# Two products of the 256-token matmuls in one instruction of 512 moving columns

## The chip, the cores and the metric

The kernel runs on one core of a Trainium2 chip. The metric is the device time of one execution in microseconds (us). Before the change the median of three timed executions is 2486.03 us (2485.91 to 2488.45). Differences within 0.2% (about 5 us) are taken as no change.

## The reference

A model of two blocks on 256 tokens, all in float32. The first block (`first_block`) is attention over 8 heads beside a pooled branch, an output projection, and a feed-forward part with a causal convolution of width 3. The second block puts 16 meta tokens ahead of the 256 (272 in all) for an "even" layer (a state-space branch and a convolution branch), and has an "odd" layer of neighbourhood attention.

```
h = rms_norm(x, attn_norm_g)                      # 256 tokens, width 2048
proj = h @ w_in                                   # q, k, v and p
a = moba_attention(q, k, v, rel_bias)
m = multiscale_pool(p, pool_w, pool_scale)
x = x + concatenate([a, m]) @ w_out

u = rms_norm(x, ffn_norm_g) @ w_up                # 2048 -> 2 * 5632
y = conv_b + sum(conv_w[i] * shifted(u, i))       # three taps
gate, val = split(y)
x = x + (silu(gate) * val) @ w_down               # 5632 -> 2048
...
x = even layer on 272 tokens; x = odd layer: queries and gates of 256 tokens, keys and values of 272
```

## The kernel before

Activations are kept transposed: features on the 128 partitions, tokens along the free axis. So a projection to 128 output features is a sum over feature tiles k (16 for a width of 2048, 11 for a quarter of the feed-forward width) of W_k^T x_k, where the 128x128 weight tile stands in TensorE and the tokens (256 or 272 columns) move through it.

Float32 precision is kept with two parts: each factor is a sum of a high and a low part of type f32r. `split_act` makes the parts of an activation, `xh` (ScalarE copy) and `xl` (VectorE subtraction), in two tiles from a pool of 79 slots (`slot`). `split_next` makes the parts of the weights, `wH` (ScalarE, L184) and `wL` (L185, on GpSimd for the first half of most chunks, else on VectorE). `products` then issues three matmuls for each k into one accumulator: wH with xh (L225), wH with xl (L226), wL with xh (L227). The fourth product, of both low parts, is left out.

The weights stream in a fixed order (`plan`), one chunk for each 128 outputs. Three chunks are in flight in SBUF and four half chunks of parts exist, so the split of the half chunk that comes three ahead waits until TensorE is through with one. Accumulators (`acc`) rotate through three PSUM banks. What follows a chunk reads its accumulator on VectorE: in the feed-forward part `u = acc * r` (L589), then ScalarE makes `y` (L591) and VectorE adds two taps (L592, L594); for the `val` half the product with the gate (L603) and the split for the next projection (L263, L264). The down and output projections add the accumulator to the residual (L571, L621, L1104).

Chunks with 256 moving columns are: p (8 chunks), the pooled products `mix` (16 k in all), w_out (16), gate and val (88), down (64 of 11 k each), oq, oz and o_out (16 each). The q, k and v chunks of the attention have the tokens as weights (`rows`), and the whole even layer and ok, ov of the odd layer move 272 columns. A scheduling layer puts each engine's instructions in order ahead of time, engine by engine, with the code's order as priority and a model of its own for what is ready; each engine runs its list strictly in that order. In the even layer much work runs "in the background" between the chunks.

Of the kernel before, what the change touches and what calls it, by code (L numbers as in the profile page):

```python
# [10 lines left out]
F32 = mybir.dt.float32  # L11
# [23 lines left out]
# columns of the per-feature parameters  # L35
# [10 lines left out]
# columns of the phases' constants  # L46
# [11 lines left out]
class Kernel:  # L58
    def __init__(self, ctx, tc, A, out):
        self.ctx, self.tc, self.nc, self.A, self.out = ctx, tc, tc.nc, A, out  # L60
        self.bg = deque()
        self.live = []
# [8 lines left out]
    # ---------------------------------------------------------------- tiles  # L71
    NSLOT = 79
    WIDE = 5

    def slot(self, dt=F32, name="slot"):
        return self.ap_.tile([P, S2], dt, name=name, tag="slot", bufs=self.NSLOT)

# [11 lines left out]

    def gp(self):  # L90
        return self.pp.tile([P, 512], F32, name="gp", tag="gp", bufs=3)
# [10 lines left out]
    # ------------------------------------------------------- weight streaming  # L102
# [55 lines left out]
    def load_next(self, parts=1):  # L158
        """the next chunk; yields before each of its parts."""
# [10 lines left out]
    def split_next(self):  # L170
        """the next piece of the weights as two f32r parts whose sum is exact."""
# [26 lines left out]
    def chunk(self, key, ahead=1):  # L198
# [6 lines left out]
        while self.n_split < min(i + 1 + ahead, n):  # L205
            # ahead of the work in the background, where there is much of it
# [1036 lines left out]
```

## Time and profile before

| | |
|---|---|
| median of three timed executions | 2486.03 us (2485.91 to 2488.45) |
| span of the profiled execution, first to last instruction | 2484.6 us |
| TensorE matmul (PE) busy | 2422.9 us (98%) |
| VectorE (DVE) busy | 1681.3 us (68%) |
| ScalarE (ACT) busy | 1254.7 us (50%) |
| GpSimd (POOL) busy | 1092.7 us (44%) |
| mean granted TensorE clock | 0.988 |

The page does not time what lies around the span; the median of the timed executions is 1.4 us above the span. Busy time of PE counts any stretch in which a matmul is in the array; matmuls overlap in it, so a busy PE can still be made faster by fewer or denser matmuls.

### The profile page before, as it was taken

How to read it: one execution, taken by the hardware profiler on the slowest of the kernel's cores; microseconds unless marked ns; L12 is line 12 of the kernel's file. 1: busy time of each engine (PE TensorE's matmuls, PEld its weight loads, DVE VectorE, ACT ScalarE, POOL GpSimd, SP SyncE). 2: the span in 40 equal slices, each digit the busy share in tenths (PEclk: the TensorE clock that was granted, in tenths of full speed). 3: DMA queues.
4: the chain of work that ended last, by engine and by line, in shares of the span. 5: the costliest groups of instructions: out<-in, count | busy, mean ns of one | idle time of the engine just before them, and what ended most of it. 6: DMA issues, size and time to landing. Idle time of an engine off the chain costs nothing. (4 is left out here: it accounts for less than half of the span.)

```text
span 2484.6 us, 48431 instructions
## 1 busy us (share of the span) xinstructions
PE 2422.9 (98%) x19742; PEld 2379.5 (96%) x19742; DVE 1681.3 (68%) x2917; ACT 1254.7 (50%) x1914; POOL 1092.7 (44%) x505
## 2 busy tenths in 40 slices
PE   8999999999999999999989998988999999999998
PEld 8998999999999999999989997878999999999998
DVE  6566466667666667889999988888767644443443
ACT  6564455554554554554445564744544444444553
POOL 1133444445445445644458765444334333333443
PEclk9999999999999999999999998999999999999999
DMA  8545655557657656865545464554666544444553
GB/s 284 185 140 195 231 192 184 182 176 231 219 175 228 224 177 223 256 206 176 171 146 194 168 205 146 183 165 151 214 231 211 187 157 169 171 167 170 197 187 119
DMA packets 116415, 471.62 MB, mean 190 GB/s; under 512 B 17376, under 2 KB 54496, under 8 KB 72416
## 3 DMA queue, kind: packets, MB, share of 16 engines
q1 hardware_dynamic: 94880, 443.87, 53.4%
q10 hardware_dynamic: 21312, 24.67, 2.8%
q8 instruction: 154, 2.52, 0.4%
q14 instruction: 69, 0.57, 0.1%
HBM read 448.94 MB, written 19.54 MB: 189 GB/s over the span
## 5 line engine op out<-in xcount | busy, mean ns | idle before, releaser
L225 PE MATMUL acc<-xh,wH 128*128 128x256 f32 (+1 forms) x5856 | 1678.1, 287 | 17.8 <-DVE c L755 8.9
L227 PE MATMUL acc<-xh,wL 128*128 128x256 f32 (+1 forms) x5856 | 1669.1, 285 | 2.7 <-POOL wL L185 2.4
L226 PE MATMUL acc<-xl,wH 128*128 128x256 f32 (+1 forms) x5856 | 1671.6, 285 | 0.2 <-DVE xl L267 0.2
L185 POOL TENSOR_TENSOR wL<-raw,wH 128x1024 fp32r<-128x1024 f32 (+1 forms) x435 | 1041.2, 2396 | 1316.0 <-ACT wH L184 1212.2
L184 ACT ACTIVATE wH<-raw 128x1024 fp32r<-128x1024 f32 (+1 forms) x838 | 832.7, 998 | 854.3 <-PE acc L226 641.8
L225 PEld LDWEIGHTS acc<-xh,wH 128*128 128x128 f32 x5856 | 1110.0, 190 | 27.2 <-ACT dt L739 9.1
L227 PEld LDWEIGHTS acc<-xh,wL 128*128 128x128 f32 x5856 | 1109.0, 189 | 4.8 <-POOL wL L185 4.0
L226 PEld LDWEIGHTS acc<-xl,wH 128*128 128x128 f32 x5856 | 1109.2, 189 | 1.2 <-DVE xl L267 0.3
L185 DVE TENSOR_TENSOR wL<-raw,wH 128x1024 fp32r<-128x1024 f32 (+2 forms) x403 | 579.6, 1440 | 142.1 <-ACT wH L184 137.1
L665 DVE SCALAR_TENSOR_TENSOR cvp<-u,prm,cvp 128x264 f32<-128x264 f32 (+14 forms) x480 | 210.0, 488 | 0.3
L264 DVE TENSOR_TENSOR xl<-y,xh 128x256 fp32r<-128x256 f32 x44 | 98.7, 2243 | 25.0 <-ACT xh L263 25.0
L238 PE MATMUL acc<-wH,xh 128*128 128x256 f32 x384 | 108.6, 285 | 5.8 <-ACT xh L266 5.8
L589 DVE TENSOR_TENSOR u<-acc,r 128x256 f32<-128x256 f32 x88 | 36.7, 418 | 111.2 <-PE acc L227 109.1
L240 PE MATMUL acc<-wH,xl 128*128 128x256 f32 x384 | 108.9, 285 | 0.9 <-DVE xl L267 0.9
L239 PE MATMUL acc<-wL,xh 128*128 128x256 f32 x384 | 107.5, 282 | 0.0
L238 PEld LDWEIGHTS acc<-wH,xh 128*128 128x128 f32 x384 | 72.8, 190 | 5.8 <-ACT xh L266 5.8
L290 DVE TENSOR_TENSOR nacc<-nacc,sq 128x272 f32<-128x272 f32 (+1 forms) x103 | 70.9, 688 | 9.8 <-ACT sq L279 8.6
L240 PEld LDWEIGHTS acc<-wH,xl 128*128 128x128 f32 x384 | 72.8, 190 | 2.3 <-DVE xl L267 1.9
L849 POOL TENSOR_TENSOR e<-e 128x128 f32<-128x128 f32 x64 | 47.8, 769 | 57.3 <-DVE e L847 55.4
L239 PEld LDWEIGHTS acc<-wL,xh 128*128 128x128 f32 x384 | 72.6, 190 | 0.1
L761 DVE SCALAR_TENSOR_TENSOR gp<-c,prm,gp 128x270 f32<-128x270 f32 (+1 forms) x128 | 62.9, 496 | 3.3 <-ACT gp L757 3.1
L621 DVE TENSOR_TENSOR xw<-acc,xw 128x256 f32<-128x256 f32 x64 | 27.2, 424 | 51.3 <-PE acc L227 48.6
(231 smaller groups left out, 1456.7 us busy)
## 6 DMA issues: line engine op xcount, KB each, us to landing
raw<-in_e_w_in_dram SPq DMA_DIRECT2D x97, 1024.0 KB
raw<-in_w_up_dram SPq DMA_DIRECT2D x88, 1024.0 KB
raw<-in_o_w_in_dram SPq DMA_DIRECT2D x64, 1024.0 KB
raw<-in_w_down_dram SPq DMA_DIRECT2D x64, 704.0 KB
raw<-in_e_w_out_dram SPq DMA_DIRECT2D x32, 1024.0 KB
raw<-in_w_qkv_dram SPq DMA_DIRECT2D x21, 1024.0 KB
raw<-in_w_out_dram SPq DMA_DIRECT2D x16, 1024.0 KB
raw<-in_o_w_out_dram SPq DMA_DIRECT2D x16, 1024.0 KB
```

What stands on the lines that cost most here:

```text
L184: nc.scalar.activation(H[:, c], w[:, c], AF.Copy)
L185: eng.tensor_tensor(L[:, c], w[:, c], H[:, c].bitcast(F32), op=OP.subtract)
L225: nc.tensor.matmul(ps, wh, xh, start=k == 0, stop=False)
L226: nc.tensor.matmul(ps, wh, xl, start=False, stop=False)
L227: nc.tensor.matmul(ps, wl, xh, start=False, stop=k == n - 1)
L238: nc.tensor.matmul(ps[b], xh, H[:, o:o + 256], start=k == 0, stop=False)
L239: nc.tensor.matmul(ps[b], xh, L[:, o:o + 256], start=False, stop=False)
L240: nc.tensor.matmul(ps[b], xl, H[:, o:o + 256], start=False, stop=k == 15)
L264: nc.vector.tensor_tensor(l, x, h.bitcast(F32), op=OP.subtract)
L290: nc.vector.tensor_tensor(st["acc"], st["acc"], sq, op=OP.add)
L665: nc.vector.scalar_tensor_tensor(cps[i][:, a:b], u[i][:, a + s:b + s], self.prm_("dww", k * 16 + i), cps[i][:, a:b], op0=OP.mult, op1=OP.add)
L761: nc.vector.scalar_tensor_tensor(y[:, a:b], t[:, a + d:b + d], self.prm_("ecw", k * 32 + c), y[:, a:b], op0=OP.mult, op1=OP.add)
```

## The change

The two parts of an activation now lie in one tile of two halves (`twin`, [128, 2, 272]). With 256 tokens the matmul of wH takes both halves as its moving operand, 512 columns, and writes the two halves of a PSUM bank (`acc2`); the matmul of wL with the high part adds 256 columns to the first half. The halves are added when the result is read (`add2`): a ScalarE copy of the second half and a VectorE addition of the first, or, where a residual is added anyway, two VectorE additions. The form with 272 tokens stays at three matmuls, since 544 columns don't fit a bank. Tiles of one part share a twin by twos (`slot`), and the pool has 39 twins (78 halves) in place of 79 slots.

```diff
-    NSLOT = 79
+    NSLOT = 39
-    def slot(self, dt=F32, name="slot"):
-        return self.ap_.tile([P, S2], dt, name=name, tag="slot", bufs=self.NSLOT)
+    def twin(self, dt=F32, name="twin"):
+        return self.ap_.tile([P, 2, S2], dt, name=name, tag="slot", bufs=self.NSLOT)
+    def slot(self, name="slot"):
+        if self.half is None:
+            t = self.twin(name=name)
+            self.half = t[:, 1]
+            return t[:, 0]
+        t, self.half = self.half, None
+        return t
+    def acc2(self):
+        return self.pp.tile([P, 2, S1], F32, name="acc", tag="acc", bufs=3)
...
-            xh, xl = pairs[k]
+            x = pairs[k]
             wh, wl = self.weights(W, k if at is None else at[k])
-            nc.tensor.matmul(ps, wh, xh, start=k == 0, stop=False)
-            nc.tensor.matmul(ps, wh, xl, start=False, stop=False)
-            nc.tensor.matmul(ps, wl, xh, start=False, stop=k == n - 1)
+            if len(ps.shape) == 3:
+                nc.tensor.matmul(ps, wh, x, start=k == 0, stop=False, skip_group_check=True)
+                nc.tensor.matmul(ps[:, 0], wl, x[:, 0], start=False, stop=k == n - 1, skip_group_check=True)
+            else:
+                nc.tensor.matmul(ps, wh, x[:, 0], start=k == 0, stop=False)
+                nc.tensor.matmul(ps, wh, x[:, 1], start=False, stop=False)
+                nc.tensor.matmul(ps, wl, x[:, 0], start=False, stop=k == n - 1)
+    def add2(self, out, ps, x=None):
+        nc = self.nc
+        if x is None:
+            nc.scalar.copy(out, ps[:, 1])
+        else:
+            nc.vector.tensor_tensor(out, ps[:, 1], x, op=OP.add)
+        nc.vector.tensor_tensor(out, ps[:, 0], out, op=OP.add)
...
-        h = self.slot(F32R, "xh")[:, :n]
-        l = self.slot(F32R, "xl")[:, :n]
+        t = self.twin(F32R, "xhl")[:, :, :n]
+        h, l = t[:, 0], t[:, 1]
...
-                ps = self.acc()[:, :S1]
+                ps = self.acc2()
                 self.products(ps, W, [mixed[2 * g], mixed[2 * g + 1]], [4 * (g % 2) + j, 4 * (g % 2) + 2 + j])
-                mX[2 * g + j] = self.split_act(ps, S1, self.prm_("pscale", 2 * g + j))
+                t = self.work("mx")[:, :S1]
+                self.add2(t, ps)
+                mX[2 * g + j] = self.split_act(t, S1, self.prm_("pscale", 2 * g + j))
...
-            ps = self.acc()[:, :S1]
+            ps = self.acc2()
             self.products(ps, W, X)
             u = self.work("u")[:, :S1]
-            nc.vector.tensor_tensor(u, ps, r(), op=OP.mult)
+            self.add2(u, ps)
+            nc.vector.tensor_tensor(u, u, r(), op=OP.mult)
...
-                ps = self.acc()[:, :S1]
+                ps = self.acc2()
                 self.products(ps, W, K)
                 x = t[:, NM:]
-                nc.vector.tensor_tensor(x, ps, x, op=OP.add)
+                self.add2(x, ps, x)
```

p, oq and oz change as the feed-forward `u` does, w_out and o_out as the down projection.

TensorE's list, in a chunk of the feed-forward part, two of its 16 k before the change (names are out<-in with buffer numbers):

```order
L225 MATMUL acc_5859<-xh_2948,wH_5785 128x256
L226 MATMUL acc_5859<-xl_2949,wH_5785 128x256
L227 MATMUL acc_5859<-xh_2948,wL_5786 128x256
L225 MATMUL acc_5859<-xh_3027,wH_5785 128x256
L226 MATMUL acc_5859<-xl_3028,wH_5785 128x256
L227 MATMUL acc_5859<-xh_3027,wL_5786 128x256
```

The same place after it, three k (line numbers are those of the changed kernel: L242 and L243 stand in `products`):

```order
L242 MATMUL acc_4889<-xhl_2769,wH_4826 128x512
L243 MATMUL acc_4889<-xhl_2769,wL_4827 128x256
L242 MATMUL acc_4889<-xhl_2832,wH_4826 128x512
L243 MATMUL acc_4889<-xhl_2832,wL_4827 128x256
L242 MATMUL acc_4889<-xhl_2886,wH_4826 128x512
L243 MATMUL acc_4889<-xhl_2886,wL_4827 128x256
```

Each k has two matmuls in place of three, with as many columns in all.

VectorE's list in the feed-forward part, from the read of one val accumulator to the next gate's, before:

```order
L589 TENSOR_TENSOR u_5908<-acc_5859,r_4071 128x256
L185 TENSOR_TENSOR wL_5926<-raw_5849,wH_5925 128x1024
L592 SCALAR_TENSOR_TENSOR y_5910<-u_5908,prm_72,y_5910 128x255
L594 SCALAR_TENSOR_TENSOR y_5910<-u_5908,prm_72,y_5910 128x254
L603 TENSOR_TENSOR y_5910<-y_5844,y_5910 128x256
L264 TENSOR_TENSOR xl_5916<-y_5910,xh_5915 128x256
L589 TENSOR_TENSOR u_5978<-acc_5929,r_4071 128x256
```

And after the change, for a val chunk as well (L256 adds in `add2`, L622 is the product with r, L199 the weights' low part, L625 and L627 the taps, L636 the product with the gate, L293 the split):

```order
L256 TENSOR_TENSOR u_4974<-acc_4941,u_4974 128x256
L622 TENSOR_TENSOR u_4974<-u_4974,r_3637 128x256
L625 SCALAR_TENSOR_TENSOR y_4978<-u_4974,prm_72,y_4978 128x255
L627 SCALAR_TENSOR_TENSOR y_4978<-u_4974,prm_72,y_4978 128x254
L636 TENSOR_TENSOR y_4978<-y_4926,y_4978 128x256
L199 TENSOR_TENSOR wL_5045<-raw_4986,wH_5044 128x1024
L293 TENSOR_TENSOR xhl_4983<-y_4978,xhl_4983 128x256
L256 TENSOR_TENSOR u_5029<-acc_4996,u_5029 128x256
```

There is one more addition a chunk, the product with r now has both inputs in SBUF, and the weights' low part has moved from ahead of the taps to behind the product with the gate.

ScalarE's list in the even layer where the background of the state-space branch starts, before (c5 are results of the convolutions of width 5, here the last of x; cb, x0 and xt belong to the first group):

```order
L930 DMA z_a3_18377<-z_a_18375 128x272
L831 COPY cb_18398<-gp_18399 128x16
L952 ACTIVATE xw_21264<-xw_21264 128x272
L817 ACTIVATE x0_18394<-x0_18392 128x128
L764 ACTIVATE c5_18048<-gp_18042 128x272
L859 COPY xt_18411<-gp_18408 128x256
L184 ACTIVATE wH_18553<-raw_18436 128x1024
```

And after the change:

```order
L864 COPY cb_16018<-gp_16019 128x16
L892 COPY xt_16031<-gp_16028 128x256
L198 ACTIVATE wH_16176<-raw_16056 128x1024
L797 ACTIVATE c5_15594<-gp_15588 128x272
L797 ACTIVATE c5_15594<-gp_15663 128x272
L892 COPY xt_16145<-gp_16142 128x256
```

Both of the last two c5 tiles, which share a twin, are now written behind the first group; before, one was.

## Rows read from the trace of the kernel before

**Rows 1.** The page: busy time, and TensorE's granted clock in 40 slices.

```profile
span 2484.6 us, 48431 instructions
...
PE 2422.9 (98%) x19742; PEld 2379.5 (96%) x19742; DVE 1681.3 (68%) x2917; ACT 1254.7 (50%) x1914; POOL 1092.7 (44%) x505
...
PEclk9999999999999999999999998999999999999999
```

**Rows 2.** Groups of matmuls by line and shape: count, busy us, mean ns, idle before.

```profile
L226 PE MATMUL acc<-xl,wH 128*128 128x256 f32 x3280 | 925.2, 282 | 0.2 <-DVE xl L267 0.2
L225 PE MATMUL acc<-xh,wH 128*128 128x256 f32 x3280 | 924.3, 282 | 8.8 <-ACT xh L266 6.3 <-DVE xl L267 1.9 <-DVE p L538 0.5
L227 PE MATMUL acc<-xh,wL 128*128 128x256 f32 x3280 | 923.1, 281 | 0.1
```

**Rows 3.** Windows, PE alone: us, busy, matmuls, granted clock, DMA share.

```profile
400.00:980.00 580.00, 580.00 (x4900) 1.00 0.60 201
1120.00:1240.00 120.00, 120.00 (x962) 1.00 0.50 170
```

**Rows 4.** Timeline of PE in the feed-forward part: start, us.

```profile
600.10 0.28 PE L227 MATMUL acc<-xh,wL 128*128 128x256 f32 x1
600.22 0.29 PE L225 MATMUL acc<-xh,wH 128*128 128x256 f32 x1
600.34 0.28 PE L226 MATMUL acc<-xl,wH 128*128 128x256 f32 x1
600.46 0.27 PE L227 MATMUL acc<-xh,wL 128*128 128x256 f32 x1
```

**Rows 5.** PE's own waits, the longest: us in total, times, longest.

```profile
PE gp L857 <- DVE c L878: 11.6, 2, 6.5
PE acc L225 <- DVE c L755: 8.9, 1, 8.9
PE acc L225 <- ACT xh L266: 6.3, 2, 3.4
PE gp L813 <- DVE dupx L811: 5.4, 1, 5.4
PE acc L225 <- DVE xl L267: 1.9, 2, 1.4
```

**Rows 6.** Windows, all engines: PE, PEld, DVE, ACT, POOL busy; gate and val, then down.

```profile
434.80:496.90 62.10, 62.10 (x526) 62.10 (x525) 42.19 (x55) 32.77 (x44) 25.92 (x12) 1.00 0.53 182
559.00:618.00 59.00, 59.00 (x502) 59.00 (x501) 41.53 (x37) 24.44 (x33) 34.42 (x15) 1.00 0.70 224
```

**Rows 7.** Groups of VectorE by line and shape, whole span.

```profile
L589 DVE TENSOR_TENSOR u<-acc,r 128x256 f32<-128x256 f32 x88 | 36.7, 418 | 111.2 <-PE acc L227 109.1 <-ACT r L308 2.1
L264 DVE TENSOR_TENSOR xl<-y,xh 128x256 fp32r<-128x256 f32 x44 | 98.7, 2243 | 25.0 <-ACT xh L263 25.0
L603 DVE TENSOR_TENSOR y<-y 128x256 f32<-128x256 f32 x44 | 19.3, 439 | 3.3 <-ACT y L601 1.8
L185 DVE TENSOR_TENSOR wL<-raw,wH 128x384 fp32r<-128x384 f32 x64 | 139.4, 2178 | 6.0 <-ACT wH L184 2.0
L185 DVE TENSOR_TENSOR wL<-raw,wH 128x256 fp32r<-128x256 f32 x16 | 6.2, 416 | 5.0 <-ACT wH L184 5.0
```

**Rows 8.** Timelines of DVE and of POOL in the gate and val chunks.

```profile
479.15 2.42 DVE L264 TENSOR_TENSOR xl<-y,xh 128x256 fp32r<-128x256 f32 x1 [0.59 <-ACT xh L263]
481.50 0.41 DVE L589 TENSOR_TENSOR u<-acc,r 128x256 f32<-128x256 f32 x1
...
486.37 0.42 DVE L589 TENSOR_TENSOR u<-acc,r 128x256 f32<-128x256 f32 x1 [2.42 <-PE acc L227]
...
478.89 2.40 POOL L185 TENSOR_TENSOR wL<-raw,wH 128x1024 fp32r<-128x1024 f32 x1 [3.29 <-ACT wH L184]
484.58 2.41 POOL L185 TENSOR_TENSOR wL<-raw,wH 128x1024 fp32r<-128x1024 f32 x1 [3.29 <-ACT wH L184]
```

**Rows 9.** Groups of ScalarE by line and shape: a copy out of PSUM, the weights' split.

```profile
L422 ACT COPY q<-acc 128x256 f32<-128x256 f32 x8 | 3.0, 372 | 8.4 <-PE acc L240 8.4
L184 ACT ACTIVATE wH<-raw 128x1024 fp32r<-128x1024 f32 x750 | 790.5, 1057 | 842.7 <-PE acc L226 633.8 <-issue 151.9 <-PE acc L240 22.6
```

**Rows 10.** Timeline at the end: the last accumulator's addition on DVE.

```profile
2472.76 0.42 DVE L1104 TENSOR_TENSOR x<-acc,x 128x256 f32<-128x256 f32 x1 [5.27 <-PE acc L227]
2474.10 0.38 DVE L328 TENSOR_SCALAR ms<-gp 128x1 f32<-128x1 f32 x2 [0.92 <-PE gp L325]
```

**Rows 11.** Windows in the even layer, all engines as in Rows 6.

```profile
1242.30:1304.40 62.10, 53.19 (x421) 53.00 (x421) 60.99 (x108) 26.22 (x33) 32.18 (x13) 0.96 0.42 146
1490.80:1552.90 62.10, 53.53 (x361) 47.78 (x361) 52.52 (x97) 27.07 (x46) 33.32 (x23) 0.89 0.43 146
```

More of the change, by code (lines that the diff above doesn't have):

```diff
@@ L61, in __init__ @@
         self.bg = deque()
+        self.half = None
         self.live = []
@@ L236, in rows @@
             for b in blocks:
-                xh, xl = (t[:, b * P:(b + 1) * P] for t in X[k])
+                xh, xl = (X[k][:, i, b * P:(b + 1) * P] for i in range(2))
                 nc.tensor.matmul(ps[b], xh, H[:, o:o + 256], start=k == 0, stop=False)
@@ L267, in split_act @@
             nc.vector.scalar_tensor_tensor(l, x, scale, h.bitcast(F32), op0=OP.mult, op1=OP.subtract)
-        return h, l
+        return t
     def norm_begin(self, n, tail=0):
@@ L537, in attention @@
             p = self.work("p")[:, :S1]
-            nc.vector.tensor_tensor(p, ps, rf, op=OP.mult)
+            self.add2(p, ps)
+            nc.vector.tensor_tensor(p, p, rf, op=OP.mult)
             self.advance()
@@ L552, in attention @@
         K = [aX[h] for h in range(HEADS)] + [mX.get(k - 8) for k in at[8:]]
-        first = self.acc()[:, :S1]
+        first = self.acc2()
         self.products(first, W, K, at, range(10))
@@ L585, in conv @@
             W = self.chunk((kind, i))
-            ps = self.acc()[:, :S1]
+            ps = self.acc2()
             self.products(ps, W, X)
             u = self.work("u")[:, :S1]
-            nc.vector.tensor_tensor(u, ps, r(), op=OP.mult)
+            self.add2(u, ps)
+            nc.vector.tensor_tensor(u, u, r(), op=OP.mult)
             y = self.work("y")[:, :S1]
@@ L617, in down @@
                 W = self.chunk(("down", s, j))
-                ps = self.acc()[:, :S1]
+                ps = self.acc2()
                 self.products(ps, W, K)
                 x = t[:, NM:]
-                nc.vector.tensor_tensor(x, ps, x, op=OP.add)
+                self.add2(x, ps, x)
                 if last:
@@ L873, in pair @@
             m = slice(32 * i, 32 * i + 32)
-            (xh, xl), (wh, wl) = X0[t], W0[t]
+            (xh, xl), (wh, wl) = X0[t], (W0[t][:, j] for j in range(2))
             for n, (a, b) in enumerate(((xh, wh), (xh, wl), (xl, wh))):
@@ L995, in odd @@
         negm = cols(cd, CD, "neg").rearrange("p (b k) -> p b k", b=2)
-        XG = [(h[:, NM:], l[:, NM:]) for h, l in X]
+        XG = [t[:, :, NM:] for t in X]
         rg = lambda: r()[:, NM:]
@@ L1059, in odd @@
             W = self.chunk(("oq", hp))
-            ps = self.acc()[:, :S1]
+            ps = self.acc2()
             self.products(ps, W, XG)
@@ L1063, in odd @@
             q = self.work("oq")[:, :S1]
-            nc.vector.scalar_tensor_tensor(q, ps, 0.125, rg(), op0=OP.mult, op1=OP.mult)
+            self.add2(q, ps)
+            nc.vector.scalar_tensor_tensor(q, q, 0.125, rg(), op0=OP.mult, op1=OP.mult)
             kv = []
@@ L1079, in odd @@
             W = self.chunk(("oz", i))
-            ps = self.acc()[:, :S1]
+            ps = self.acc2()
             self.products(ps, W, XG)
@@ L1083, in odd @@
             t = self.work("oz")[:, :S1]
-            nc.vector.tensor_tensor(t, ps, rg(), op=OP.mult)
+            self.add2(t, ps)
+            nc.vector.tensor_tensor(t, t, rg(), op=OP.mult)
             nc.scalar.activation(t, t, AF.Silu)
@@ L1100, in odd @@
             W = self.chunk(("o_out", j))
-            ps = self.acc()[:, :S1]
+            ps = self.acc2()
             self.products(ps, W, K)
             nc.sync.dma_start(x[j], self.x[j][:, NM:])
-            nc.vector.tensor_tensor(x[j], ps, x[j], op=OP.add)
+            self.add2(x[j], ps, x[j])
             self.norm_add(st, x[j])
```

## The prediction

> **What bounds the kernel now.** I read the page first, then TensorE's groups, its windows, its waits, and last the engines beside it. The page shows TensorE's matmuls in progress during 98% of the span, at a granted clock of full level (the upper one of 1.2 and 2.4 GHz) in nearly every slice, while VectorE has 32% of the span free, ScalarE 50% and GpSimd 56% [rows 1]. That PE is busy says little, since matmuls overlap; the two views that count are PE's waits and its step. The waits come to few microseconds: the five longest are 34 us in all, and most of these stand in the even layer [rows 5], which the change leaves at three matmuls. So in the stages with 256 columns TensorE issues one matmul after another without a stop, and the time of such a stage is the number of matmuls by the step between their starts.
>
> The step can be read from windows without waits. In the feed-forward part 4900 matmuls of 256 columns fill 580 us: 118.37 ns each. In the even layer's first part 962 of 272 columns fill 120 us: 124.74 ns [rows 3]. The two differ by 6.37 ns for 16 columns, so 0.398 ns a column, and a part is left that doesn't depend on the columns: 118.37 - 256 x 0.398 = 16.5 ns. The shorter window is uncertain by one matmul, 0.13 ns, which moves the slope by 0.008. If the slope is one cycle of the 2.4 GHz level, 0.417 ns, the fixed part is 118.37 - 106.7 = 11.7 ns by the first window and 124.74 - 113.3 = 11.4 ns by the second. I take 11.6, nearest to both windows at the granted clock, and keep 16.5 as the upper bound. The duration of a row (282 ns, [rows 2]) is the way of one matmul through the array and no step.
>
> The fixed part doesn't come from the change of weights: L225 and L226 use the same wH tile one after the other, L227 another, and each step in the timeline is 0.12 us [rows 4].
>
> **What the change removes.** Each of the 3280 k of the 256-token products [rows 2] has three matmuls of 256 columns, 3 x 118.4 = 355.1 ns, and will have one of 512 and one of 256. The columns stay; one fixed part of three goes. A 512-column matmul has no row. Between the bounds: nothing saved (236.7 ns, two steps of 256) and 16.5 ns saved. By the fixed part of 11.6 it steps 213.3 + 11.6 = 224.9 ns, a k takes 343.3 ns, and the sum is 3280 x 11.6 = **38.0 us** (0 to 54 us). It lies on the path that sets the end, since these stages have hardly a wait. A chunk of 16 k goes from 5.68 to 5.49 us, one of 11 from 3.91 to 3.78.
>
> The Trainium skill bears on this (TensorE: Matmul & The Clock Gate, Back-to-back issue gap): it gives a back-to-back gap of columns by cycle plus about 2.5 ns. The rows show 11.4 to 16.5 instead, in a stream where each matmul has its own weight load; by the page's 2.5 ns the saving would be 3280 x 2.5 = 8.2 us.
>
> **What it adds.** ScalarE gets 136 copies out of PSUM (8 p, 8 mix, 88 gate and val, 16 oq, 16 oz) at 0.37 us [rows 9], 50 us. VectorE gets an addition for each of these and for the 96 residual chunks (16 + 64 + 16): 232 by 0.42 us, the price of L589, which also reads PSUM [rows 7], 97 us. ScalarE would stand at 53% of the new span, VectorE at 73%. What hides them is the three-bank ring: an accumulator read out late holds TensorE up only if its bank isn't free two chunks later, 11 us for gate and val and 7.6 us for down, while the longer chain is 0.37 + 0.42 us longer. Without that cover each of the 136 would cost 0.8 us, 108 us.
>
> The order shows one thing more. `y` on ScalarE waits for the product with r, and behind it in the list stands the split of the next weights. In the order after the change the first half chunk's split stands ahead of `y`, and the second behind it; before, `y` came first. The weights are three half chunks ahead, 8 us, against 1.1 us on ScalarE and 2.4 us on GpSimd, so a stall of 2 us there stays hidden.
>
> **GpSimd beside VectorE.** The edit with the greatest risk is small: the product with r had one input in PSUM, and now has two in SBUF. Such an instruction can meet GpSimd. L264 takes 2243 ns in the feed-forward part, L603, of the same form and size, 439 [rows 7]; L264 starts at 479.15 while GpSimd's wL runs from 478.89 to 481.29, and the next VectorE instruction starts at 481.50 [rows 8]. So a VectorE subtraction from two SBUF tiles was held until GpSimd was through. The Trainium skill says so as a rule (SBUF — State Buffer, Who interferes with whom): a VectorE instruction with two SBUF inputs contends with a GpSimd instruction that reads SBUF, and the later one waits; the trace agrees, with 2243 against 439 ns.
>
> What can it cost? For a gate or val chunk of 5.68 us VectorE is busy 3.85 us (42.19 of 62.1), of which 0.90 is L264's hold in every other chunk; GpSimd runs 2.37 us [rows 6]. Without holds VectorE needs 2.95, with the new addition 3.37. It can't be held longer than GpSimd runs, so 5.74 us is the ceiling, against a chunk of 5.49: at most 0.25 x 88 = 22 us. For down, where L185 of 384 columns is held today (2178 ns against 416 for 256 columns), the same sum gives 3.85 against 3.78, 64 x 0.07 = 4.5 us. So 0 to 26 us. I take nothing: the product with r comes about 2 us behind the end of a chunk (ScalarE's split 1.06, copy 0.37, addition 0.42; [rows 7, 9]), and GpSimd runs from 1.7 us before the end to 0.7 us behind it (484.58 to 486.99 against VectorE's u at 486.37) [rows 8], so they miss each other, and L264 moves clear of it too.
>
> **Small terms.** At the pooled products (`mix`) PE waits for the split out of the accumulators, 6.3 + 1.9 us at four places [rows 5]. Their chain grows by a copy and an addition, 0.8 us; on the other hand the bank is free when these two have read it, not when the split has. Bounds -2 and +3.2 us, taken +1.5. At the end one addition stands behind the last matmul [rows 10]: +0.4. The even layer keeps its matmuls, and its list on TensorE keeps its places but for a few around the first group: 0, with ±6 us for waits that shift there.
>
> **Sum.** Span 2484.6 - 38.0 + 1.5 + 0.4 = 2448.5 us; with the 1.4 us by which the median lies above the span, **2450 us**.
>
> **Rivals.**
> - *GpSimd holds VectorE after all* (10%): half the ceiling, 13 us, gives 2463; all of it 2476. For it speaks that L264 and L185 are held today; against it the phase above.
> - *The even layer's background is held up* (8%). Twins pair lifetimes: both last c5 tiles wait for the first group, and each holds one of the three gp banks meanwhile. PE's waits at that place are 5.4 and part of 11.6 us [rows 5], in a window with 53.5 of 62.1 us busy; another such window is limited by VectorE, 61.0 of 62.1 [rows 11]. If the waits there double, +12 us: 2462.
> - *Only part of the fixed piece goes* (4%): half of it, 5.8 ns a k by the step of [rows 3], 19 us in all, gives 2469 us. By the Trainium skill's 2.5 ns a k it would be 2480.
> - *Nothing goes* (4%): the second half of the moving operand starts like a matmul of its own, at 236.7 ns. 2488 us, no change.
> - *Slower* (6%): the wide matmul reads two stretches of SBUF 272 elements apart and fills a whole bank, which no row here does. If the passage costs a second fixed part, it steps 248.3 ns, 3280 x 11.6 = 38 us are lost, and the time is 2526. The point: above 236.1 ns the change loses, above 237.7 it loses over 0.2%. Against it: source and destination are contiguous within each half, as today.
>
> **How the numbers follow.** The forecast (68%) is 2450 us, by itself 2441 to 2458 (the fixed part by a nanosecond either way is 3.3 us, the even layer 6). The range 2436 to 2468 takes in the upper bound of the fixed part nearly, the even layer's rival and the first half of GpSimd's; outside lie the other three, 14%, and tails. Faster by over 0.2% (5 us, about what a measurement tells from no change): 68 + 10 + 8 + 4 = 90%. Same 4%, slower 6%.
>
> **What would show it.** In the changed kernel a window of the feed-forward part should hold 2 matmuls per 343 ns (338 to 355 decides the cause), the 272-column window still 124.7 ns. L622 (product with r) should stay near 0.42 us and L293 of y fall below 2 us; if they read 2 us and PE shows waits for acc or wL there, GpSimd's rival is right. New PE waits around the first group would be the twins. I am wrong if a k still takes 355 ns.

## The result and the profile after

The changed kernel takes 2654.23 us (median of 4 runs, 2651.74 to 2656.84) against 2486.64 us: ratio 1.0673, 95% interval 1.066 to 1.0686. It is 168 us slower; the forecast was 2450. The span of the profiled execution goes from 2484.6 to 2650.0 us, so the whole loss stands inside the profile.

The page of the changed kernel, engines' busy time and two of its rows of slices:

```profile
PE 2470.0 (93%) x16462; PEld 2228.4 (84%) x16462; DVE 1889.8 (71%) x3149; ACT 1280.0 (48%) x2048; POOL 1096.7 (41%) x505
...
PE   8999998888988898878998999998999999999988
...
PEclk9999999999999999999999999998999999999999
```

Against [rows 1], TensorE is no longer without a stop: most slices of the feed-forward part (the 6th to the 19th) read 8 or 7, at the full clock. No other engine is near its limit. So TensorE waits, and for engines that are idle themselves. TensorE's waits in the changed kernel (what waits, for what; total, times, longest), the first six:

```profile
PE acc L243 <- POOL wL L199: 51.9, 60, 1.9
PE acc L243 <- DVE wL L199: 26.6, 37, 0.8
PE acc L242 <- ACT wH L198: 22.4, 34, 1.5
PE gp L890 <- DVE c L911: 11.2, 2, 6.5
PE acc L245 <- DVE c L788: 8.3, 1, 8.3
PE acc L242 <- DVE xhl L293: 8.0, 3, 5.4
```

The first three are new ([rows 5] had none of them among the longest): TensorE waits for parts of the weights. The groups that say why, of all engines:

```profile
L199 POOL TENSOR_TENSOR wL<-raw,wH 128x1024 fp32r<-128x1024 f32 (+1 forms) x435 | 1041.6, 2397 | 1475.0 <-ACT wH L198 1426.3
...
L622 DVE TENSOR_TENSOR u<-u,r 128x256 f32<-128x256 f32 x88 | 195.1, 2218 | 4.7 <-ACT r L337 1.8
L624 ACT ACTIVATE y<-u,prm 128x256 f32<-128x256 f32 x88 | 52.9, 601 | 225.9 <-DVE u L622 225.9
L625 DVE SCALAR_TENSOR_TENSOR y<-u,prm,y 128x255 f32<-128x255 f32 x88 | 46.1, 524 | 60.5 <-ACT y L624 60.5
```

The same activation `y` on ScalarE before the change:

```profile
L591 ACT ACTIVATE y<-u,prm 128x256 f32<-128x256 f32 x88 | 52.2, 594 | 14.8 <-DVE u L589 14.7
```

The product with r takes 2218 ns where it took 418 [rows 7]; `y` waits 226 us for it, where it waited 15, and GpSimd waits 1426 us for wH, where it waited 1212.

The stages, in us, from the start of each stage's first product matmul to that of the next (worked out from the trace's starts; "up" is the 88 gate and val chunks in four stages, the second of which begins at 457.79 us and ends at 608.20):

| | before | after | e1 | e2 | e3 | e4 | e5 | e6 | e8 | e11 | e12 |
|---|---|---|---|---|---|---|---|---|---|---|---|
| to the end of w_out | 314.9 | 318.8 | 317.9 | 322.4 | 326.2 | 322.9 | 323.1 | 319.2 | 317.9 | 314.6 | 321.0 |
| up, four stages | 501.2 | **574.0** | 494.0 | 571.9 | 574.0 | 492.1 | 492.1 | 492.1 | 500.8 | 492.1 | 492.1 |
| down, first three | 187.1 | **239.2** | 231.0 | 201.2 | 238.3 | 193.0 | 195.6 | 195.3 | 188.2 | 197.9 | 222.8 |
| down, the last | 62.1 | **84.7** | 84.7 | 75.6 | 84.3 | 75.6 | 61.3 | 61.3 | 62.8 | 62.8 | 84.7 |
| even layer | 878.5 | 882.2 | 885.8 | 883.3 | 883.1 | 883.0 | 882.2 | 878.8 | 883.6 | 880.5 | 884.8 |
| oq, ok, ov, oz | 437.7 | 438.2 | 437.3 | 437.0 | 439.3 | 438.3 | 437.2 | 436.7 | 437.9 | 437.2 | 438.3 |
| o_out | 90.6 | 99.6 | 99.7 | 100.5 | 101.5 | 99.7 | 99.7 | 93.1 | 90.4 | 89.3 | 99.8 |
| tail | 12.4 | 13.2 | 13.2 | 12.9 | 13.2 | 13.4 | 13.3 | 12.7 | 12.3 | 13.1 | 13.2 |

Of the 165 us, 73 are lost in up, 75 in down, 9 in o_out, and 4 each in the even layer and up to the end of w_out. Two stages in the windows view (length; busy time and matmuls of PE; granted clock; DMA share; GB/s), the second up and the first down:

```profile
457.80:608.20 150.40, 134.21 (x707) 1.00 0.42 150
608.20:688.06 79.86, 66.89 (x354) 0.98 0.61 197
```

352 k in 150.4 us are 427 ns each. Where nothing waits, a k is faster than before. Steps of the changed kernel in the timeline of PE (start, duration), to be set against [rows 4]:

```profile
601.42 0.40 PE L242 MATMUL acc<-xhl,wH 128*128 128x512 f32 x1
601.65 0.28 PE L243 MATMUL acc<-xhl,wL 128*128 128x256 f32 x1
601.77 0.39 PE L242 MATMUL acc<-xhl,wH 128*128 128x512 f32 x1
602.00 0.28 PE L243 MATMUL acc<-xhl,wL 128*128 128x256 f32 x1
602.12 0.39 PE L242 MATMUL acc<-xhl,wH 128*128 128x512 f32 x1
```

0.35 us a k; over all starts of the trace the wide step is 231 ns and the narrow one 118 ns in the median, 349 together, against 355.1 before.

**The loop in up.** Two chunks of the second up stage, the lists of VectorE, ScalarE and GpSimd one below the other (in brackets the idle time ahead, and what ended it):

```profile
482.77 2.35 DVE L622 TENSOR_TENSOR u<-u,r 128x256 f32<-128x256 f32 x1
485.79 0.48 DVE L625 SCALAR_TENSOR_TENSOR y<-u,prm,y 128x255 f32<-128x255 f32 x1 [0.67 <-ACT y L624]
...
489.09 2.60 DVE L622 TENSOR_TENSOR u<-u,r 128x256 f32<-128x256 f32 x1
...
485.15 0.60 ACT L624 ACTIVATE y<-u,prm 128x256 f32<-128x256 f32 x1 [2.79 <-DVE u L622]
485.66 1.04 ACT L198 ACTIVATE wH<-raw 128x1024 fp32r<-128x1024 f32 x1
487.28 0.42 ACT L292 ACTIVATE xhl<-y 128x256 fp32r<-128x256 f32 x1 [0.58 <-DVE y L636]
487.61 0.36 ACT L253 COPY u<-acc 128x256 f32<-128x256 f32 x1
487.86 1.06 ACT L198 ACTIVATE wH<-raw 128x1024 fp32r<-128x1024 f32 x1
491.72 0.60 ACT L624 ACTIVATE y<-u,prm 128x256 f32<-128x256 f32 x1 [2.80 <-DVE u L622]
...
498.82 0.60 ACT L624 ACTIVATE y<-u,prm 128x256 f32<-128x256 f32 x1 [2.79 <-DVE u L622]
...
482.43 2.40 POOL L199 TENSOR_TENSOR wL<-raw,wH 128x1024 fp32r<-128x1024 f32 x1 [4.71 <-ACT wH L198]
489.00 2.41 POOL L199 TENSOR_TENSOR wL<-raw,wH 128x1024 fp32r<-128x1024 f32 x1 [4.17 <-ACT wH L198]
```

Read it from 487.61: the copy out of the accumulator, behind it at once wH (to 488.92), behind that GpSimd's wL (489.00 to 491.41). The product with r starts at 489.09, 0.09 us behind wL, and ends only at 491.69. `y` follows at 491.72, and the next wH stands behind `y` in ScalarE's list. So does the next copy: after a val chunk it stands behind the split (L292), which waits for the product with the gate, and that for the taps and `y`. No step of this circle waits for TensorE. Two chunks take 498.82 - 485.15 = 13.67 us, and TensorE needs 32 x 0.349 = 11.2 of them. 11 such pairs by 2.5 us are the 27 us that this stage takes beyond 122.9 (the length without stops, e4). It is the slowest of the four; the others take 139.0, 142.4 and 142.3 us.

**The loop in down.** There is no product with r in down, and its chunks take 4.75 us in the steady part in place of 3.89. The timeline of two chunks in the first down stage, VectorE, ScalarE (ACTq is its queue of DMA issues) and GpSimd; L255 and L256 are the two additions of one residual in `add2`:

```profile
632.43 0.41 DVE L255 TENSOR_TENSOR xw<-acc,xw 128x256 f32<-128x256 f32 x1
634.50 2.43 DVE L199 TENSOR_TENSOR wL<-raw,wH 128x384 fp32r<-128x384 f32 x1 [1.66 <-ACT wH L198]
636.86 0.41 DVE L256 TENSOR_TENSOR xw<-acc,xw 128x256 f32<-128x256 f32 x1
637.19 0.41 DVE L255 TENSOR_TENSOR xw<-acc,xw 128x256 f32<-128x256 f32 x1
639.25 2.42 DVE L199 TENSOR_TENSOR wL<-raw,wH 128x384 fp32r<-128x384 f32 x1 [1.66 <-ACT wH L198]
...
632.99 1.47 ACT L198 ACTIVATE wH<-raw 128x1024 fp32r<-128x1024 f32 x2 [3.27 <-DVE xw L255]
637.30 0.33 ACTq L385 DMA_DIRECT2D x<-xw  x1
637.75 1.47 ACT L198 ACTIVATE wH<-raw 128x1024 fp32r<-128x1024 f32 x2 [3.28 <-DVE xw L255]
...
634.13 2.39 POOL L199 TENSOR_TENSOR wL<-raw,wH 128x1024 fp32r<-128x1024 f32 x1 [2.37 <-ACT wH L198]
638.88 2.38 POOL L199 TENSOR_TENSOR wL<-raw,wH 128x1024 fp32r<-128x1024 f32 x1 [2.37 <-ACT wH L198]
```

The scheduling layer has put the 384-column wL between the two additions (632.43 and 636.86). The circle: wH (632.99), GpSimd's wL (634.13), VectorE's wL held until GpSimd is through (634.50 to 636.93), the second addition (636.86 to 637.27), the store on ScalarE (637.30), and only then the next wH (637.75): 4.76 us. The label "L255" on ScalarE's idle time is not what it waited for: the store stands ahead of wH, and starts as the second addition ends.

### The profile page after: what moved, and what is told of

The parts are those of the page before. It is cut to its first block, busy times and chain, and to the rows that moved or that the text cites. A ratio compares the mean times of both kernels' runs of the same rounds, so it can differ in the third digit from the quotient of the medians.

```text
span 2650.0 us, 42399 instructions
## 1 busy us (share of the span) xinstructions
PE 2470.0 (93%) x16462; PEld 2228.4 (84%) x16462; DVE 1889.8 (71%) x3149; ACT 1280.0 (48%) x2048; POOL 1096.7 (41%) x505
## 5 line engine op out<-in xcount | busy, mean ns | idle before, releaser
L199 POOL TENSOR_TENSOR wL<-raw,wH 128x1024 fp32r<-128x1024 f32 (+1 forms) x435 | 1041.6, 2397 | 1475.0 <-ACT wH L198 1426.3
L242 PE MATMUL acc<-xhl,wH 128*128 128x512 f32 x3280 | 1174.0, 398 | 43.6 <-ACT wH L198 22.4
L243 PE MATMUL acc<-xhl,wL 128*128 128x256 f32 x3280 | 942.2, 287 | 82.8 <-POOL wL L199 51.9
L199 DVE TENSOR_TENSOR wL<-raw,wH 128x1024 fp32r<-128x1024 f32 (+2 forms) x403 | 582.1, 1447 | 319.4 <-ACT wH L198 313.7
L242 PEld LDWEIGHTS acc<-xhl,wH 128*128 128x128 f32 x3280 | 621.0, 189 | 194.0 <-ACT wH L198 33.3
L245 PE MATMUL acc<-xhl,wH 128*128 128x272 f32 x2576 | 754.9, 293 | 8.4 <-DVE c L788 8.3
L247 PE MATMUL acc<-xhl,wL 128*128 128x272 f32 x2576 | 749.2, 291 | 2.5 <-POOL wL L199 2.4
L246 PE MATMUL acc<-xhl,wH 128*128 128x272 f32 x2576 | 747.0, 290 | 0.2 <-DVE xhl L296 0.2
L243 PEld LDWEIGHTS acc<-xhl,wL 128*128 128x128 f32 x3280 | 623.0, 190 | 132.9 <-POOL wL L199 79.8
L245 PEld LDWEIGHTS acc<-xhl,wH 128*128 128x128 f32 x2576 | 490.3, 190 | 14.0 <-ACT dt L772 8.5
L246 PEld LDWEIGHTS acc<-xhl,wH 128*128 128x128 f32 x2576 | 492.6, 191 | 1.9 <-issue 1.0
L247 PEld LDWEIGHTS acc<-xhl,wL 128*128 128x128 f32 x2576 | 490.1, 190 | 3.9 <-POOL wL L199 3.4
L622 DVE TENSOR_TENSOR u<-u,r 128x256 f32<-128x256 f32 x88 | 195.1, 2218 | 4.7 <-ACT r L337 1.8
L267 PE MATMUL acc<-wH,xhl 128*128 128x256 f32 x384 | 109.6, 287 | 6.5 <-ACT xhl L295 6.3
L268 PE MATMUL acc<-wL,xhl 128*128 128x256 f32 x384 | 109.0, 285 | 0.9 <-DVE wL L199 0.8
L269 PE MATMUL acc<-wH,xhl 128*128 128x256 f32 x384 | 108.3, 283 | 0.3 <-DVE xhl L296 0.3
L625 DVE SCALAR_TENSOR_TENSOR y<-u,prm,y 128x255 f32<-128x255 f32 x88 | 46.1, 524 | 60.5 <-ACT y L624 60.5
L267 PEld LDWEIGHTS acc<-wH,xhl 128*128 128x128 f32 x384 | 73.1, 191 | 6.8 <-ACT xhl L295 6.3
L295 ACT ACTIVATE xhl<-xw,prm 128x272 fp32r<-128x272 f32 (+1 forms) x48 | 24.9, 518 | 108.2 <-DVE xw L1015 54.7
```

The costliest lines, as they stand in the source:

```text
L199: eng.tensor_tensor(L[:, c], w[:, c], H[:, c].bitcast(F32), op=OP.subtract)
L242: nc.tensor.matmul(ps, wh, x, start=k == 0, stop=False, skip_group_check=True)
L243: nc.tensor.matmul(ps[:, 0], wl, x[:, 0], start=False, stop=k == n - 1, skip_group_check=True)
L245: nc.tensor.matmul(ps, wh, x[:, 0], start=k == 0, stop=False)
L246: nc.tensor.matmul(ps, wh, x[:, 1], start=False, stop=False)
L247: nc.tensor.matmul(ps, wl, x[:, 0], start=False, stop=k == n - 1)
```

## The experiments

Where no interval stands, the time is that of one execution. The first theory: two closed loops of waits, one in up through the product with r and `y`, one in down through the second addition and the store. The rivals: the added work itself, or the wide matmul.

**e1: the sum goes back into the accumulator (up only).**

```diff
-            self.add2(u, ps)
-            nc.vector.tensor_tensor(u, u, r(), op=OP.mult)
+            self.add2(u, ps, back=True)      # ps[:, 0] += copy of ps[:, 1]
+            nc.vector.tensor_tensor(u, ps[:, 0], r(), op=OP.mult)
```

> In the feed-forward part the sum of the two halves is written back into the accumulator, and the product with r reads it there: it has one SBUF input, as before the change. The lists of ScalarE and GpSimd stay as in the changed kernel. Theory (a loop of waits: GpSimd's wL holds the product with r on VectorE, y on ScalarE waits for that, the next wH stands behind y, and wL behind wH): the product falls from 2.2 to about 0.42 us, the four gate/val stages fall from 574 us together to 490 to 520, the down stages stay at 324, the whole is 2575 to 2600 us. First rival (the added copy and addition, or the order on ScalarE, are the cost with or without the hold): within 15 us of 2654. Second rival (the hold only passes on to the taps L625 and L627, which read two SBUF tiles): they read 2 us in the mean, and the whole is above 2630.

2565.39 us. Two groups of VectorE in this kernel:

```profile
L622 DVE TENSOR_TENSOR u<-acc,r 128x256 f32<-128x256 f32 x88 | 37.3, 424 | 4.7 <-ACT r L337 1.8
L625 DVE SCALAR_TENSOR_TENSOR y<-u,prm,y 128x255 f32<-128x255 f32 x88 | 114.2, 1298 | 60.5 <-ACT y L624 60.5
```

With as much work as after and the same lists on ScalarE and GpSimd, up falls from 574.0 to 494.0 us. Down stays slow. Part of the hold does pass on to the tap L625 (1298 ns in place of 524), as the second rival said, but that instruction stands behind `y`, and the circle now has room for it. The gain, 89 us, is more than the theory's 54 to 79: 80 stand in up, as expected, and 8 in the first three down stages (231.0 in place of 239.2), which were expected to stay.

**e2: the stores of down on SP's queue.**

```diff
-                    self.x_store(j, t)
+                    self.x_store(j, t, NM, nc.sync)
```

> Only the store of the residual in the down stages is issued from SP's queue in place of ScalarE's; VectorE's and GpSimd's lists stay as in the changed kernel. Theory (in down a second loop of waits, without the product with r: VectorE's list has the 384-column wL between the two additions of a residual, the store on ScalarE waits for the second addition, the next wH stands behind the store, and wL waits for wH): the four down stages fall from 324 us to 245 to 252, the gate/val stages stay at 574, the whole is 2575 to 2585 us. Rival (GpSimd's hold of the 384-column wL and the added work on VectorE set the pace of down): the down stages stay above 310, the whole above 2640.

2606.58 us. Down falls from 323.9 to 276.8 us and up stays, so the store is a link of the circle; but 245 to 252 was expected. The first three stages stand at 67 us, the last at 75.6. In the steady part of the first three a chunk takes 3.83 us (VectorE's first additions start at 640.59, 644.42 and 648.25), although the wL still stands between the two additions and still takes 2.4 us. So the rival (GpSimd's hold and the added work set the pace whatever the store does) is wrong there. The theory is not complete: in the last stage a circle is left without the store (e4, e5).

**e3: three matmuls of 256 into the two halves.**

```diff
-                nc.tensor.matmul(ps, wh, x, start=k == 0, ...)
+                nc.tensor.matmul(ps[:, 0], wh, x[:, 0], start=k == 0, ...)
+                nc.tensor.matmul(ps[:, 1], wh, x[:, 1], start=False, ...)
```

> Three matmuls of 256 columns again, into the two halves of the accumulator, so that everything behind TensorE is as in the changed kernel. Theory (the loss comes from how the accumulators are read out, not from the wide matmul): gate/val stays at 565 to 580 us in four stages, down at 320 to 328, the whole is 2645 to 2670 us, slower than the changed kernel by what the wide matmul saves in the stages that TensorE bounds. Rival (the wide matmul itself starves TensorE, or splits late): at most 2520 us.

2662.15 us. Up takes 574.0 us with either form of matmul, and down 322.6 against 323.9. What TensorE issues doesn't matter there: the loss is made by the reading out.

**e4: both edits, of e1 and of e2, in one kernel.**

> The first two edits together: product with r out of the accumulator in the feed-forward part, and the store of down on SP's queue. Theory (two separate loops, one in each kind of stage): the gains add, 2654 less about 70 less about 75, so 2495 to 2525 us, with about 10 us still lost in the stages oz and o_out. Rival (one common cause, GpSimd's hold, that finds another place): above 2560 us.

2519.11 us (2516.91 to 2520.15), ratio 1.0124 (1.0107 to 1.0141). The gains add; the second up stage stands at 122.9 us. The last down stage shows the third way round, in the timeline of VectorE, ScalarE and GpSimd in this kernel:

```profile
1042.61 2.42 DVE L199 TENSOR_TENSOR wL<-raw,wH 128x384 fp32r<-128x384 f32 x1 [0.49 <-ACT wH L198]
1044.95 0.41 DVE L256 TENSOR_TENSOR xw<-acc,xw 128x256 f32<-128x256 f32 x1
...
1045.40 0.52 ACT L295 ACTIVATE xhl<-xw,prm 128x272 fp32r<-128x272 f32 x1 [2.82 <-DVE xw L256]
1045.83 0.42 ACT L308 ACTIVATE sq<-xw 128x272 f32<-128x272 f32 x1
1046.15 1.46 ACT L198 ACTIVATE wH<-raw 128x1024 fp32r<-128x1024 f32 x2
```

Here it is the split of the next activations (L295), not the store, that waits on ScalarE for the second addition with the next wH behind it: 5.02 us a chunk.

**e5: e1, and all wL of down on GpSimd.**

```diff
-    POOL = {..., "down": 1, ...}
+    POOL = {..., "down": 2, ...}
```

> As the run with the product with r read from the accumulator (2565 us), and in the down stages the wL of 384 columns goes to GpSimd with the other one; the store stays on ScalarE. So nothing stands between the two additions of a residual on VectorE, and GpSimd has 2.4 + 0.9 us of work in a chunk of 3.83. Theory (the loop of down closes over the wL between the two additions, whatever waits for the second one on ScalarE): all four down stages, the last one too, take 61 to 64 us in place of 76 to 85, the whole 2493 to 2505 us. Rival (GpSimd's rate, or the store on ScalarE by itself, paces down): down stays above 66 us a stage, the whole above 2515.

2506.27 us, 1 us above the range. The last down stage takes 61.3 us in place of 84.7, with the store where it was: it is the wL between the two additions that closes the circle. Its hold alone is not new: it takes 2219 ns in the changed kernel and took 2178 before [rows 7], at 3.89 us a chunk. The first three keep 64.5 to 66.3 us, more than the 61 to 64 expected.

**e6: e5, with the sum in the accumulator for p, mix, oq and oz too.** The edit of e1 at four more places, for oz:

```diff
-            self.add2(t, ps)
-            nc.vector.tensor_tensor(t, t, rg(), op=OP.mult)
+            self.add2(t, ps, back=True)
+            nc.vector.tensor_tensor(t, ps[:, 0], rg(), op=OP.mult)
```

> As the kernel before it in this group, and the product with r of p, oq and oz and the split of the pooled products read the sum from the accumulator too, so that no instruction behind an added accumulator has two SBUF inputs because of the change. Theory (the 9 us lost in o_out and part of the 3 to 6 us in p and mix are the same hold): o_out falls from 99.6 to about 91 us, and the whole is 2483 to 2493 us, equal to the kernel before the change within 0.3%. Rival (these are the price of the longer chain at the change from one stage to the next): within 3 us of the kernel before it in this group.

2492.57 us (2485.00 to 2497.03), ratio 1.002 (1.0011 to 1.0029). o_out falls from 99.7 to 93.1 us: the hold was there too, in the product with r of oz, which took 1986 ns in the changed kernel and takes 424 here:

```profile
L1119 DVE TENSOR_TENSOR oz<-oz,r 128x256 f32<-128x256 f32 x16 | 31.8, 1986 | 0.5
```

In p the product with r was held as well (1152 ns in the changed kernel), but no gain is shown there. The time to the end of w_out falls from 323.1 us in e5 to 319.2, but it is 318.8 in the changed kernel; from 150 to 325 us TensorE stands at its lower clock for 17.1 us in e5, 10.2 here and 6.8 in the changed kernel. The ten times follow the granted clock too, from 2485.00 us at 0.989 to 2497.03 at 0.984. A window of the second up stage in this kernel:

```profile
446.50:568.50 122.00, 122.00 (x700) 1.00 0.50 177
```

700 matmuls in 122 us without a gap: 348.6 ns a k. This is what the wide matmul gives, 9.1 us over the four up stages.

**e7: e6 with the halves of an activation next to each other.**

```diff
-        t = self.twin(F32R, "xhl")[:, :, :n]
+        t = self.ap_.tile([P, 2 * S2], F32R, name="xhl", ...)[:, :2 * n].rearrange("p (a b) -> p a b", a=2)
```

> As the one with all sums in the accumulator, but the two halves of an activation lie next to each other (512 columns without a gap; oq and oz keep their offset form, 512 of the 3280 k). Theory one (the jump of 16 columns inside the moving operand costs the 6 ns by which the wide step, 231 ns, lies above columns and one fixed part): the wide step falls to about 225 ns and the whole by 2768 x 6 = 17 us, to 2466 to 2476 us. Theory two (the wide step is 231 whatever the spacing): within 4 us of the one with all sums in the accumulator.

2493.05 us (2484.23 to 2496.97), ratio 1.0019 (1.0009 to 1.003); the steps stay at 231 and 117 to 118 ns. The jump of 16 columns costs nothing.

**e8: the pairing of tiles alone**, on the kernel before.

> The kernel before the change with its tiles paired (39 twins in place of 79 slots), and nothing else of the change: three matmuls into one accumulator, one read. If the pairing alone is behind the 3.6 us that the even layer loses, the even layer takes 881 to 884 us in place of 878.6 and the whole 2488 to 2493 us; if not, both are within 1.5 us of before. The other stages stay as before the change either way.

2493.21 us (2490.06 to 2496.02), ratio 1.0027 (1.0016 to 1.0038). The even layer takes 883.6 us in this profile and 882.2 after, but 878.8 in e6 with the same pairing. So the pairing costs some 6 us in the whole. The profile of one run has 5 of them in the even layer, but not as waits: TensorE waits there for 35.1 us, 35.8 before the change. What grows is its time at the lower clock, from 41.0 to 51.2 us. Whether the pairing does that, or this one execution, isn't shown.

**e9: e6 with wide matmuls alone** (the products with the low parts of the weights are left out).

```diff
-                nc.tensor.matmul(ps[:, 0], wl, x[:, 0], start=False, stop=k == n - 1, ...)
```

> As the kernel with all sums in the accumulator, but the matmul of wL is left out (the low parts of the weights don't count), so that wide matmuls follow one another. Read is only the step between starts where TensorE doesn't wait, not the whole time. Theory one (the wide matmul has a fixed part of about 18 ns of its own): 231 ns from wide to wide. Theory two (the 6 ns above columns and the usual 11.6 ns come from the change between a wide and a narrow matmul): 225 ns.

The median step from wide to wide is 233 ns (69 starts without a wait from 580.11 to 595.94 us: 15.83 / 68 = 0.233). Theory one holds: the wide matmul has a larger fixed part of its own.

**e10: e6, the first three chunks of down with the 384-column wL on VectorE.**

```diff
+        if key[0] == "down" and key[2] < 3:
+            return piece < 1
```

> As the kernel with all sums in the accumulator, but in the first three chunks of each down stage the wL of 384 columns stays on VectorE, so that GpSimd doesn't have six wL in a row (10 us) at the change from up to down. Theory (the 3.2 us that each of the first three down stages still loses there, 64.5 us against 61.3 in the last, is GpSimd's backlog): these stages take 61.5 to 63 us and the whole is 5 to 9 us less than with all sums in the accumulator. Rival (with the wL between the two additions again, the first three chunks are late by as much): the stages stay at 64 us or more.

2500.14 us (2498.96 to 2502.97), ratio 1.0053 (1.0039 to 1.0067). The stages take 65.5 to 67.1 us: the rival is right, and taking the backlog off GpSimd doesn't win the 3 us back. Since the edit puts a wL between the two additions again, it doesn't tell whether the backlog is their cause.

**e11: wide only in up, w_out and o_out**, with the sum in the accumulator for up; the rest as before the change, for down:

```diff
-                ps = self.acc2()
+                ps = self.acc()[:, :S1]
...
-                self.add2(x, ps, x)
+                nc.vector.tensor_tensor(x, ps, x, op=OP.add)
```

> The wide matmul only in gate/val (with the sum in the accumulator), w_out and o_out; p, mix, down, oq and oz with three matmuls and one read as before the change. Theory (each k saves 6.6 ns where nothing else waits): the four gate/val stages take 492 us in place of 501, down 249 as before, o_out about 89; with the 6 us that the pairing alone cost, the whole is 2475 to 2485 us, ratio to before 0.996 to 0.999. Rival (the longer chain of reading out costs as much elsewhere): 2486 us or more.

2490.45 us (2485.70 to 2492.34), ratio 1.0012 (1.0003 to 1.0021). Up takes 492.1 us as expected and o_out 89.3, but down takes 197.9 for the first three stages, 10.8 more than before the change with the same instructions. The pairing of tiles is not the reason (e8: 188.2).

**e12: the changed kernel, with all wL of gate and val on VectorE.**

```diff
-    POOL = {..., "gate": 1, "val": 1, ...}
+    POOL = {..., "gate": 0, "val": 0, ...}
```

> The changed kernel with all wL of gate and val on VectorE; the product with r keeps its two SBUF inputs. Theory (the product takes 2.2 us because GpSimd runs beside it): it takes about 0.43 us, and the four gate/val stages fall from 574 to 492 to 510 us although VectorE gets 1.2 us more work a chunk; the whole is 2572 to 2600 us. Rival (two SBUF inputs are slow by themselves, or a read of the sum just written is): the product stays above 1.5 us and the stages above 560 us.

2558.34 us, 14 below the range: up is where it was expected, and the first three down stages fall too, from 239.2 to 222.8 us, which no theory here explains. The product with r in this kernel:

```profile
L622 DVE TENSOR_TENSOR u<-u,r 128x256 f32<-128x256 f32 x88 | 37.4, 426 | 3.4 <-ACT r L337 0.5
```

The same instruction, with both inputs in SBUF, takes 426 ns when GpSimd is idle, and up takes 492.1 us although VectorE has more to do. The hold is GpSimd's.

**e13 and e14: the change from up to down**, both on e11: e13 with three matmuls in the last pair of chunks of each quarter, e14 with both wL of the third chunk of down on VectorE.

```diff
+            two = i % SLAB < SLAB - 1                      # e13
+            ps = self.acc2() if two else self.acc()[:, :S1]
...
+        if key[0] == "down" and key[2] == 2:               # e14
+            return False
```

> As the kernel with the wide matmul where it pays, but the last gate and val chunk of each quarter have three matmuls and one read, so that the work at the change from up to down stands as before the change. Theory (the 3 us that each down stage loses there come from the gate product of the last val chunk, held 2.6 us by GpSimd because the chain behind the wide matmul is 0.8 us later): the first three down stages take 62.3 us again in place of 65.3 to 67.2, and the whole is 8 to 10 us less than where it pays, about 2481 us. Rival (the loss is that of a faster stage that runs into the same limit of the weights' split): down stays at 65 us.

> As the kernel with the wide matmul where it pays, but both wL of the third chunk of each down stage go to VectorE, so that GpSimd is idle where the gate product of the last val chunk was held. Theory (GpSimd's hold of that product is what delays the wH behind it): the first three down stages take 62 to 63.5 us, the whole is 5 to 9 us less than where it pays. Rival (VectorE, with 1.2 us more there, is late by as much): 65 us or more.

2490.27 us (2485.91 to 2495.07), ratio 1.0017 (1.0008 to 1.0026); and 2489.14 us (2483.25 to 2491.75), ratio 1.0009 (1.0000 to 1.0018). The first three down stages take 65.0 to 67.2 us and 64.6 to 66.5. In neither is the gate product held at that place any more (2.6 us in e11), and the loss stays: my theory for it falls. Nearly all of TensorE's waits there are for GpSimd's wL (3.4 of 3.6 us in the first down stage of e11, 1.9 of 2.3 in e13). What makes the change from chunks of 5.6 to chunks of 3.9 us come out 3 us worse than before stays open.

## Why the prediction was wrong

**The step that failed is "GpSimd beside VectorE"**, in three places (the third stands in "What it adds", just ahead of it).

"I take nothing ... so they miss each other": the phase was read from the kernel before, and the change makes its own. In the paragraph above it I had read that a wH now stands ahead of `y`; it stands directly behind the copy. From that it follows that GpSimd's wL starts as that wH ends, and the product with r comes an addition behind the copy: within 0.1 to 0.4 us of each other in the rows above. e1 and e12 show the hold by two independent ways of taking it off: each brings up from 574.0 to 494.0 and 492.1 us. The Trainium skill (SBUF — State Buffer, Who interferes with whom) has it that a VectorE instruction with two SBUF inputs contends with a GpSimd instruction that reads SBUF; the runs agree with 2218, 424 (one input in PSUM) and 426 ns (no GpSimd).

"5.74 us is the ceiling": I added up VectorE's busy time and compared it with a chunk. That bounds what an engine can do, not how long a circle of waits takes. After the change VectorE is busy 71% of the span, and the circle (copy, wH, wL with the held product, `y`, wH) takes 13.67 us for two chunks with every engine idle in turn. The ceiling of 22 us for up became 73 us in the stages (82 against what the wide matmul allows).

"The weights are three half chunks ahead, 8 us ... so a stall of 2 us there stays hidden": a lead is used up once. A stall of 1.25 us in every chunk isn't hidden by a lead of 8 us but eats it, and then sets the pace.

**The loss in down was in no term and no rival.** I took down's second addition as 0.42 us behind the end of a chunk, hidden by the ring of accumulators. The ring did hide it: in down TensorE's waits are for wL and wH, none for a bank. I didn't look at where the two additions stand in VectorE's list. They aren't adjacent: between them stands a wL that waits for wH, and whatever waits for the second addition on ScalarE (the store, L385; in the last stage the split, L295) has the next wH behind it. e5 shows that it is the wL between them: 61.3 us in place of 84.7. The Trainium skill says of ScalarE's queue that it is strictly first in, first out (PSUM — Partial Sum Buffer, Engine vs sequencer instructions), so nothing passes a store that waits; the rows agree, with 3.3 us idle on ScalarE ahead of each wH in down.

**The rival "GpSimd holds VectorE after all"** (10%, 2463 to 2476 us) had the right instruction and the wrong size, and so the wrong sign; the sign that I had named for it (L622 at 2 us, waits for wL) is what the trace shows. My slower rival at 248.3 ns is refuted by the step of 231. It was also priced wrong: a second fixed part in the wide matmul gives 213.3 + 2 x 11.6 = 236.5 ns, no change; 248.3 takes a third.

**What the change removes** was mis-sized. The wide step is 231 ns, not 224.9: of a fixed part of 11.6 ns 5 to 7 go, as in the rival "only part of the fixed piece goes" (4%). A k takes 348.6 in place of 343.3 ns, and the saving without waits is 3280 x 6.5 = 21 us, not 38. e9 shows that the larger fixed part, 17 to 19 ns, belongs to the wide matmul, and e7 that the jump in its operand isn't the reason; what is stays open. That the fixed part doesn't come from the weights, as I read in [rows 4], isn't shown either: the page counts as many weight loads as matmuls (19742 each, [rows 1]), so a step without one was never seen.

**The small terms.** `mix`: from p to w_out the stages lose 2.6 us (159.4 against 156.7) where 400 k by 6.5 ns should give 2.6 back, so the longer chains cost about 5, above the bound of 3.2. By TensorE's waits they cost it behind p, where I had no term: in these stages 7.3 us are for L256, the addition that reads out p (0.5 before, for L538). My reading of [rows 5] was off as well: of its 6.3 us for xh, 2.9 stand at `mix`, and 3.4 at the start of oq (1953 us). The even layer +3.6 us, inside the ±6; no new waits stand there around the first group, as my rival had it (35.4 us of waits in all, 35.8 before). The tail +0.9 (13.25 against 12.39) for the 0.4 taken.

**Where the 21 us went once the loops were open.** In e6 up gains 9.1 us; down loses 7.4 at the changes from up (open), o_out 2.5, and the stages to the end of w_out 4.3, so that its span is 4.7 us above before. How much of this is the pairing's 6 us (e8) isn't told apart. No version here beats the kernel before: the nearest, e14, stands at 1.0009 (1.0000 to 1.0018).

## What to carry to other kernels

When an edit adds an instruction between an accumulator and what follows, write down the circle: which engine's list has the next weights' split behind an instruction that waits for the new one? Add the durations round the circle and compare with the time of a chunk; busy shares don't show it. Two instructions that belong together are not adjacent in a scheduled list, so read what stands between them, and keep an instruction that runs beside GpSimd to one SBUF input (here by leaving the sum in PSUM, with no instruction more).

## What was not expected of the hardware

Behind its longest stops TensorE runs at half its clock for a while. In the changed kernel it waits 5.4 us for xhl ahead of 2551.47 us; two windows behind that (length; PE busy and matmuls; granted clock):

```profile
2552.40:2554.40 2.00, 2.00 (x8) 0.50 0.03 8
2555.00:2557.00 2.00, 2.00 (x13) 1.00 0.52 127
```

At the lower level of 1.2 GHz a k takes 0.64 us in place of 0.35, so the four k behind this stop cost another 1.4 us. Over the whole trace of the changed kernel 34 wide steps take 0.40 to 0.48 us, 32 of them at the lower clock: by 0.29 us a k some 9 us. In the kernel before, which has no long stop there, the feed-forward part runs at the full clock throughout.

A matmul of twice the columns has a larger fixed part (17 to 19 ns above 512 columns at 0.417 ns a column, by e6 and e9; 10 to 12 ns above 256 or 272), so joining two matmuls saves less than one fixed part.
